# S5 branch of a hybrid decoder layer: halves swapped by DMA copies instead of products with a permutation, and the inner table laid out contiguously

## The chip, the cores and the metric

The kernel runs on one core of one Trainium2 chip. The metric is the device time of one execution in microseconds; several timed runs give a median. The core has five engines with queues of their own, each in order: TensorE (PE, with its weight loads as PEld), VectorE (DVE), ScalarE (ACT), GpSimd (POOL) and SyncE (SP). SP does no arithmetic here: it issues nearly all DMAs.

## What is computed

One decoder layer on 512 prompt tokens (plus 16 meta tokens in front) and 8 running sequences of 4 tokens, with model width 1024, in float32: a gated linear recurrence (HGRN2, 8 heads) and a grouped diagonal state-space branch (S5, 64 groups of 16 channels with 64 complex states each) are merged by gates, and an expert retrieval follows. The change is in the S5 branch, of which the reference says:

```
a_bar = exp(lam * delta)                      # per group and state, complex
b_bar = ((a_bar - 1.0) / lam) * (b_re + i b_im)
bu = einsum('gpc,nlgc->nlgp', b_bar, ug)      # 16 channels to 64 complex states
xs_t = a_bar * xs_(t-1) + bu_t                # a scan over the tokens
y = real(einsum('gcp,nlgp->nlgc', cc, xs)) + d_skip * ug
```

## The kernel before

The kernel works in stages, and within a stage a stream of weight tiles (class `Stream`, `run`) sets PE's order. A *job* multiplies one 128-column weight tile by all tokens: 24 steps of `gps` products (line 463) in two halves of 272 columns. After each quarter of a job (two of its eight k-steps, 12 products) `bg.tick` lets background tasks put their next step into the engines' queues. The order is thus fixed when the program is built: every engine takes its instructions in the order in which the code issues them, and waits where an operand isn't there yet or a buffer isn't free.

The weight tiles come through SP (`wraw`, two buffers). ACT makes a rounded copy `wh` of each, and POOL or DVE the remainder `wl`.

**Setup of the S5 constants** (`s5_setup`). It runs as a background task while PE does the projections and the HGRN2 heads. For each of 8 octets of groups it makes the matrices `AT` (inputs to chunk sums), `W` (states to outputs) and the block-Toeplitz table `T` (inputs to outputs within a chunk of 8 tokens). The small block `T7` is copied by 8 DMAs into a table tile of 128 x 1024 whose rows hold, per half octet, (s, c, g) with the group innermost; a DMA then stores the tile to DRAM (`Td`). Two table tiles take turns.

**The S5 units** (`s5_units`). 16 units of 4 groups each run as two background tasks, one for the even and one for the odd units; an even and an odd unit that go side by side are called a *pair* here. A unit has four steps, one tick each:

1. SP issues the loads `T`, `W`, `xs`, `xw0`, and then those of the task's next unit (`U`, `AT`, and the two rotation tables `rc` and `rs` in two halves each); PE makes `px` (line 740), ACT copies it to `X`, POOL sets up `d0`.
2. PE swaps the real and imaginary halves of the partitions of X by a product with the constant `perm` (line 755, tile `pxs`); DVE rotates (lines 760 to 762), scans over the chunks (line 767, result `z`) and starts the back rotation (line 768).
3. PE swaps the halves of z in the same way; DVE finishes the back rotation and writes the states `xs` (lines 778 to 780).
4. PE makes the outputs `py` from `U` with `T` and from `xs` with `W` (lines 785 and 786), ACT applies gelu, and ACT's queue stores `y` to DRAM (`Yd`).

`T`, `W` and `xs` have one buffer per task, `U`, `AT`, `rc` and `rs` have two. In step 4 the table is read as weights with a stride of four elements, because the group is innermost. The DMAs of SP and ACT signal their end over a set of semaphores that are used in turn; a DMA whose semaphore still belongs to an earlier DMA waits until that one has landed.

## Time and profile before

| | us |
|---|---|
| median of 3 runs | 2242.18 (2235.60 to 2245.61) |
| profiled execution, own time | 2232.85 |
| its span | 2230.7 |
| setup and heads, up to the S5 stretch | 0 to 499 |
| S5 stretch (gates and first branch products beside it) | 499 to 662 |
| the rest of the layer and the experts | 662 to 2230.7 |

Over the span PE is busy 95%, its weight loads 87%, DVE 71%, ACT 38% and POOL 36%; the chain of work that ended last runs over PE for 55% of the span and over DVE for 25%. A busy PE says little by itself, since matmuls overlap: what a product costs is read from start to start in the timeline. A row of the timeline gives the start, the time until the last of the merged instructions ended, the engine, the line, the tiles (out<-in) and the count; in brackets stand idle time before it and what ended it. A row of the windows gives the stretch, its length, the busy time of PE, PEld, DVE, ACT and POOL with instruction counts, PE's granted clock (1.00 is full speed), the DMA engines' busy share and GB/s.

### The profile page before, as it was taken

How to read it: one execution, taken by the hardware profiler on the slowest of the kernel's cores; microseconds unless marked ns; L12 is line 12 of the kernel's file. 1: busy time of each engine (PE TensorE's matmuls, PEld its weight loads, DVE VectorE, ACT ScalarE, POOL GpSimd, SP SyncE). 2: the span in 40 equal slices, each digit the busy share in tenths (PEclk: the TensorE clock that was granted, in tenths of full speed). 3: DMA queues.
4: the chain of work that ended last, by engine and by line, in shares of the span. 5: the costliest groups of instructions: out<-in, count | busy, mean ns of one | idle time of the engine just before them, and what ended most of it. 6: DMA issues, size and time to landing. Idle time of an engine off the chain costs nothing.

```text
span 2230.7 us, 34600 instructions
## 1 busy us (share of the span) xinstructions
PE 2108.4 (95%) x13085; PEld 1935.4 (87%) x13085; DVE 1587.8 (71%) x3108; ACT 848.2 (38%) x1583; POOL 811.6 (36%) x904
## 2 busy tenths in 40 slices
PE   7989999999999998999899999899999999999996
PEld 6978898898999998999799878788888888888885
DVE  6866677655335423799999678677877887787877
ACT  3323233232113323343477434333344343334343
POOL 3577762223443333564166111122222222222221
PEclk9989999999999998999999999999999999999998
DMA  5433444426644243232256989899989999888983
GB/s 151 117 96 102 127 133 139 136 99 183 193 144 129 86 154 111 91 100 72 97 227 264 333 305 344 305 333 326 332 314 325 334 335 334 307 328 309 336 302 138
DMA packets 199814, 478.90 MB, mean 215 GB/s; under 512 B 53440, under 2 KB 114752, under 8 KB 176096
## 3 DMA queue, kind: packets, MB, share of 16 engines
q1 hardware_dynamic: 169136, 278.50, 38.3%
q0 software_dynamic: 24752, 170.67, 20.7%
q10 hardware_dynamic: 5760, 27.53, 3.1%
q8 instruction: 103, 1.69, 0.3%
q14 instruction: 63, 0.52, 0.1%
HBM read 419.42 MB, written 54.46 MB: 212 GB/s over the span
## 4 chain that ended last, share of the span: by engine, by line
PE 55%; DVE 25%; issue 7%; ACT 7%; DMA 5%; POOL 1%; SPq 0%; DVEq 0%; POOLq 0%; ACTq 0%
PE gps L463 22%; PE eacc L1543 10%; DVE tlo L1472 5%; DVE uv L1348 5%; PE hps L1488 3%; PE hps L1490 3%; PE hps L1489 3%; DVE acc L1355 3%; PE pw L1423 3%; ACT thi L1464 3%; DMA traw<-in_uT 2%; PE aps L604 2%; DVE glo L477 2%; PE py L785 1%; ACT w L1350 1%
## 5 line engine op out<-in xcount | busy, mean ns | idle before, releaser
L463 PE MATMUL gps<-pr,wh 128*128 128x272 f32 (+1 forms) x3328 | 584.5, 298 | 4.4 <-DVE pr L477 3.8
L463 PEld LDWEIGHTS gps<-pr,wh 128*128 128x128 f32 x3328 | 481.9, 192 | 11.7 <-DVE pr L477 4.7
L1472 DVE TENSOR_TENSOR tlo<-traw,thi 128x1024 fp32r<-128x1024 f32 x241 | 299.1, 1241 | 139.9 <-ACT thi L1464 139.9
L1334 POOL DMA_INDIRECT uv<-in_uv,ei x128 | 176.9, 1382 | 598.4 <-DVE acc L1355 571.1
L1490 PE MATMUL hps<-pr,tlo 128*128 128x384 f32 x1024 | 348.8, 341 | 14.1 <-DVE tlo L1472 12.5
L1488 PE MATMUL hps<-pr,thi 128*128 128x384 f32 x1024 | 351.2, 343 | 8.4 <-ACT thi L1464 8.4
L463 PE MATMUL gps<-pr,wl 128*128 128x272 f32 (+1 forms) x1664 | 353.0, 292 | 1.1 <-POOL wl L429 0.7
L1489 PE MATMUL hps<-pr,thi 128*128 128x384 f32 x1024 | 345.0, 337 | 0.0
L429 POOL TENSOR_TENSOR wl<-wraw,wh 128x1024 fp32r<-128x1024 f32 x88 | 214.5, 2438 | 345.9 <-ACT wh L428 336.3
L1464 ACT CAST thi<-traw 128x1024 fp32r<-128x1024 f32 x256 | 266.0, 1040 | 37.9 <-PE eacc L1543 15.0
L463 PEld LDWEIGHTS gps<-pr,wl 128*128 128x128 f32 x1664 | 266.8, 192 | 1.7 <-POOL wl L429 1.2
L1543 PE MATMUL eacc<-thi,ghi 128*128 128x512 f32 x768 | 242.9, 397 | 6.1 <-ACT ghi L476 4.9
L1543 PE MATMUL eacc<-tlo,ghi 128*128 128x512 f32 x768 | 242.6, 397 | 4.2
L1543 PE MATMUL eacc<-thi,glo 128*128 128x512 f32 x768 | 238.1, 391 | 0.0
L1355 DVE SCALAR_TENSOR_TENSOR acc<-uv,w,acc 128x1024 f32<-128x1024 f32 x158 | 202.4, 1281 | 30.5 <-ACT w L1350 30.5
L1349 ACT ACTIVATE w<-w 128x1 f32<-128x1 f32 x160 | 32.5, 203 | 486.3 <-DVE uv L1348 486.3
L1490 PEld LDWEIGHTS hps<-pr,tlo 128*128 128x128 f32 x1024 | 193.3, 189 | 21.5 <-DVE tlo L1472 20.2
L1488 PEld LDWEIGHTS hps<-pr,thi 128*128 128x128 f32 x1024 | 193.8, 189 | 15.6 <-ACT thi L1464 10.5
L1489 PEld LDWEIGHTS hps<-pr,thi 128*128 128x128 f32 x1024 | 193.7, 189 | 3.6
L1348 DVE SCALAR_TENSOR_TENSOR uv<-uv,h 128x1024 f32<-128x1024 f32 x160 | 195.0, 1219 | 0.0
L1543 PEld LDWEIGHTS eacc<-tlo,ghi 128*128 128x128 f32 x768 | 141.2, 188 | 49.9 <-DVE tlo L1472 21.6
L1543 PEld LDWEIGHTS eacc<-thi,ghi 128*128 128x128 f32 x768 | 140.8, 188 | 42.5 <-ACT ghi L476 18.0
(403 smaller groups left out, 3026.7 us busy)
## 6 DMA issues: line engine op xcount, KB each, us to landing
traw<-in_uT SPq DMA_DIRECT2D x128, 512.0 KB
traw<-in_uv SPq DMA_DIRECT2D x128, 512.0 KB
wraw<-in_W SPq DMA_DIRECT2D x104, 512.0 KB
Wt<-wb ACTq DMA_DIRECT2D x24, 1024.0 KB
wt<-Wt SPq DMA_DIRECT2D x15, 1536.0 KB
st<-in_state_hgrn SPq DMA_DIRECT2D x8, 512.0 KB
out_o_hg_s<-st SPq DMA_DIRECT2D x8, 512.0 KB
Wd<-W SPq DMA_DIRECT2D x8, 512.0 KB
```

The costliest lines, as they stand in the source:

```text
L429: E.tensor_tensor(wl, r3, wh, ALU.subtract)
L463: mm(ps[:, b, :w], x[:, k], y[:, k, b * w : b * w + w], start=(k == 0 and x is wh and y is hi), stop=(k == KT - 1 and x is wl))
L1334: PO.indirect_dma_start(out=uvs[j], out_offset=None, in_=a["uv"], in_offset=bass.IndirectOffsetOnAxis(ap=ei[:, k : k + 1], axis=0))
L1348: V.scalar_tensor_tensor(out=uv[:, 0:D], in0=uv[:, 0:D], scalar=1.0, in1=h2, op0=ALU.mult, op1=ALU.mult, accum_out=w)
L1355: V.scalar_tensor_tensor(acc, uv[:, D:], w, acc, ALU.mult, ALU.add)
L1423: mm(pt[:, t], o2[:, t], o1[:, t], start=True, stop=True)
L1464: AC.copy(x, t)
L1472: (PO if kind == "u" and e < sum(AQ) else V).tensor_tensor(y, raws.pop((kind, e)), x, ALU.subtract)
L1488: mm(ps[:, :nt], x[:, ks], hi[:, k, cs], start=(k == 0), stop=False)
L1489: mm(ps[:, :nt], x[:, ks], lo[:, k, cs], start=False, stop=False)
L1490: mm(ps[:, :nt], y[:, ks], hi[:, k, cs], start=False, stop=(k == KT - 1))
L1543: mm(accs[d][:, b], l[:, ds_], r[:, b * 512 : b * 512 + 512], start=st, stop=en)
```

## The change

It has two parts.

- In a unit, the two products with `perm` are gone. The halves of X and of z are swapped by DMAs that SP issues, two for each (64 partitions to the other 64), into the new tiles `xw` and `zw`. The sign that `perm` carried is a per-partition constant `sgn`, applied by DVE in the multiplication with `rs`, now a scalar_tensor_tensor. The X swap is issued in step 1 behind the loads; the z swap in step 2 behind the scan.
- In the setup there is one table tile instead of two. ACT copies it into a tile `Tc` with the group outermost, and `Tc` is stored to DRAM. The load of `T` in a unit keeps its bytes, and `py` reads its weights contiguously.

```diff
-        T_["perm"] = const("perm", [P, P])
+        T_["sgn"] = const("sgn", [P, 1])
...
-        Ts = [q.tile([P, 2, 8, 16, 4], F32, name=f"T{i}") for i in range(2)]
-        for T in Ts:
-            PO.memset(T, 0.0)
+        T = q.tile([P, 2, 8, 16, 4], F32, name="T")
+        Tc = q.tile([P, 2, 4, P], F32, name="Tc")
+        PO.memset(T, 0.0)
...
         def store(o):
-            load(Td[o], Ts[o % 2].rearrange("p a s c g -> p a (s c g)"))
+            AC.copy(Tc, T.rearrange("p a s c g -> p a g (s c)"))
+            load(Td[o], Tc.rearrange("p a g n -> p a (g n)"))
...
-                load(Ts[o % 2][0 : 16 * (s + 1), :, s], T7[16 * (7 - s) : 128])
+                load(T[0 : 16 * (s + 1), :, s], T7[16 * (7 - s) : 128])
...
-            T = T.rearrange("p g n -> p (g n)").rearrange("p (n g) -> p g n", g=4)
...
             AC.copy(X, pxv)
+            xw, zw = st("xw", nch), st("zw", nch)
+
+            def swap(dst, src):
+                for x in range(2):
+                    load(dst[64 * x : 64 * x + 64], src[64 - 64 * x : 128 - 64 * x])
+
+            swap(xw, X[:, :, :nch])
...
-            yield
-
-            def swap(src):
-                t = pm.tile([P, 512], F32, name="pxs", tag="m")
-                tv = t[:, : 4 * nch].rearrange("p (g n) -> p g n", n=nch)
-                mm(tv, T_["perm"], src, start=True, stop=True)
-                return tv
-
-            xw = swap(X[:, :, :nch])
             V.tensor_tensor(Z, X[:, :, :nch], rc[:, :, 1 : nch + 1], ALU.mult)
-            V.tensor_tensor(t2, xw, rs[:, :, 1 : nch + 1], ALU.mult)
+            yield
+            V.scalar_tensor_tensor(t2, xw, T_["sgn"], rs[:, :, 1 : nch + 1], ALU.mult, ALU.mult)
...
             V.tensor_tensor_scan(z.rearrange(fl), d0.rearrange(fl), Z.rearrange(fl), 0.0, ALU.mult, ALU.add)
+            swap(zw, z)
...
-            zw = swap(z)
-            V.tensor_tensor(t2, zw, rs[:, :, 1 : nch + 1], ALU.mult)
+            V.scalar_tensor_tensor(t2, zw, T_["sgn"], rs[:, :, 1 : nch + 1], ALU.mult, ALU.mult)
```

On SP, at the third pair of units, stood before, from the odd task's load of its next `U` to the first load of the next pair:

```order
L104 DMA s_U_6158<-Ud0_103 128x328
L104 DMA s_AT_6159<-ATd_80 128x512
L104 DMA s_rc_6162<-Rd_82 64x268 x2
L104 DMA s_rs_6165<-Rd_82 64x268 x2
L104 DMA wraw_6233<-in_W 128x1024
L104 DMA s_T_6318<-Td_79 128x512
```

and stands now, from the even unit's X swap to the odd unit's z swap (`s_xw0` is a load as before, `s_xw` and `s_zw` are the swapped halves):

```order
L104 DMA s_xw_6161<-s_X_6159 64x4x66 x2
L104 DMA s_T_6174<-Td_79 128x512
L104 DMA s_W_6175<-Wd_81 128x512
L104 DMA s_xs_6176<-in_x0 128x4x8
L104 DMA s_xw0_6179<-in_x0w 128x32
L104 DMA s_U_6182<-Ud0_103 128x328
L104 DMA s_AT_6183<-ATd_80 128x512
L104 DMA s_rc_6186<-Rd_82 64x268 x2
L104 DMA s_rs_6189<-Rd_82 64x268 x2
L104 DMA s_xw_6199<-s_X_6197 64x4x66 x2
L104 DMA s_zw_6162<-s_z_6171 64x264 x2
L104 DMA s_zw_6200<-s_z_6209 64x264 x2
```

The X swap of each unit stands behind that unit's loads, and the z swaps of both units behind the X swap of the odd one.

On DVE, one pair of units reads before, from the even unit's rotation to its states:

```order
L761 TENSOR_TENSOR s_t2_6847<-pxs_6844,s_rs_6561 128x264
L762 TENSOR_TENSOR s_Z_6846<-s_Z_6846,s_t2_6847 128x264
L767 SCALAR_TENSOR_TENSOR s_z_6848<-s_d0_6799,s_Z_6846 128x264
L768 TENSOR_TENSOR s_zc_6849<-s_z_6848,s_rc_6558 128x264
L760 TENSOR_TENSOR s_Z_6876<-s_X_6838,s_rc_6599 128x264
L761 TENSOR_TENSOR s_t2_6877<-pxs_6874,s_rs_6602 128x264
L762 TENSOR_TENSOR s_Z_6876<-s_Z_6876,s_t2_6877 128x264
L767 SCALAR_TENSOR_TENSOR s_z_6878<-s_d0_6840,s_Z_6876 128x264
L768 TENSOR_TENSOR s_zc_6879<-s_z_6878,s_rc_6599 128x264
L900 SCALAR_TENSOR_TENSOR mix_5144<-mix_5144,gps_6737 128x544
L778 TENSOR_TENSOR s_t2_6847<-pxs_6912,s_rs_6561 128x264
L779 TENSOR_TENSOR s_xs_6776<-s_zc_6849,s_t2_6847 128x4x65
```

and now (the rows named SCALAR_TENSOR_TENSOR of line 766 are the scans):

```order
L760 SCALAR_TENSOR_TENSOR s_t2_6835<-s_xw_6826,c_sgn_336,s_rs_6584 128x264
L761 TENSOR_TENSOR s_Z_6834<-s_Z_6834,s_t2_6835 128x264
L766 SCALAR_TENSOR_TENSOR s_z_6836<-s_d0_6830,s_Z_6834 128x264
L768 TENSOR_TENSOR s_zc_6837<-s_z_6836,s_rc_6581 128x264
L760 SCALAR_TENSOR_TENSOR s_t2_6885<-s_xw_6876,c_sgn_336,s_rs_6634 128x264
L761 TENSOR_TENSOR s_Z_6884<-s_Z_6884,s_t2_6885 128x264
L766 SCALAR_TENSOR_TENSOR s_z_6886<-s_d0_6880,s_Z_6884 128x264
L768 TENSOR_TENSOR s_zc_6887<-s_z_6886,s_rc_6631 128x264
L899 SCALAR_TENSOR_TENSOR mix_5151<-mix_5151,gps_6764 128x544
L777 SCALAR_TENSOR_TENSOR s_t2_6835<-s_zw_6827,c_sgn_336,s_rs_6584 128x264
L778 TENSOR_TENSOR s_xs_6803<-s_zc_6837,s_t2_6835 128x4x65
```

The operations stand in the same order, but read tiles that DMAs write; the first rotation (`s_Z<-s_X`) of both units has moved ahead of this piece. As before, the even unit's states come behind the odd unit's scan.

## Rows read from the trace of the kernel before

**Rows 1.** Windows: busy us (instructions), clock, DMA share, GB/s; S5 stretch

```profile
499.00:662.00 163.00, 156.62 (x1067) 149.96 (x1065) 75.65 (x162) 35.47 (x59) 72.34 (x142) 0.98 0.59 175
```

**Rows 2.** Timeline of PE, one pair: start us, us, line, tiles, xcount

```profile
578.98 0.39 PE L786 MATMUL py<-s_xs,s_W 128*128 128x72 f32 x2
579.20 0.63 PE L785 MATMUL py<-s_U,s_T 128*128 128x72 f32 x2
579.67 0.39 PE L786 MATMUL py<-s_xs,s_W 128*128 128x72 f32 x2
...
583.62 0.75 PE L463 MATMUL gps<-pr,wh 128*128 128x272 f32 x4
584.21 0.42 PE L463 MATMUL gps<-pr,wl 128*128 128x272 f32 x2
...
585.21 1.01 PE L740 MATMUL px<-s_U,s_AT 128*128 128x82 f32 x8
...
587.60 0.61 PE L755 MATMUL pxs<-s_X,c_perm 128*128 128x264 f32 x2
587.85 0.85 PE L463 MATMUL gps<-pr,wh 128*128 128x272 f32 x4
588.54 0.41 PE L463 MATMUL gps<-pr,wl 128*128 128x272 f32 x2
```

**Rows 3.** Timeline of SP's queue: loads of one unit, start us, us

```profile
528.51 0.38 SPq L104 DMA_DIRECT2D s_T<-Td  x1
...
534.05 0.53 SPq L104 DMA_DIRECT2D s_T<-Td  x1
```

**Rows 4.** Tiles: ns min/median/max of SP's issues, first and last start

```profile
L104 SPq DMA_DIRECT2D s_rs<-Rd x32: 444/595/601, 494.8 to 633.5; - x32
...
L104 SPq DMA_DIRECT2D T<-T x64: 595/636/1508, 163.6 to 440.1; - x64
```

**Rows 5.** Chain that ended last: transfers in it; then landing of POOL's stores

```profile
502.87 3.95 DMA s_xs<-in_x
...
549.77 2.42 DMA s_rc<-Rd
...
DMA to landing us min/median/max: 1.7/1.9/2.1
```

**Rows 6.** Timeline of all engines, first pair: DVE and PE

```profile
504.94 0.43 DVE L761 TENSOR_TENSOR s_t<-pxs,s_rs 128x264 f32<-128x264 f32 x1
...
506.69 0.43 DVE L768 TENSOR_TENSOR s_zc<-s_z,s_rc 128x264 f32<-128x264 f32 x1
...
513.79 0.43 DVE L779 TENSOR_TENSOR s_xs<-s_zc,s_t 128x260 f32<-128x260 f32 x1
...
514.34 0.39 PE L786 MATMUL py<-s_xs,s_W 128*128 128x72 f32 x2
```

**Rows 7.** Timelines: SP's second `s_T` load, then PE's last pair

```profile
507.45 0.58 SPq L104 DMA_DIRECT2D s_T<-Td  x1
...
655.57 0.39 PE L786 MATMUL py<-s_xs,s_W 128*128 128x72 f32 x2
...
661.87 0.39 PE L786 MATMUL py<-s_xs,s_W 128*128 128x72 f32 x2
```

**Rows 8.** Waits in the stretch: us in total, times, longest; SP, then PE

```profile
SPq L104 <- DMA Yd<-s_y: 22.7, 9, 4.1
...
PE pxs L755 <- DVE s_z L767: 4.6, 7, 1.3
```

**Rows 9.** Timeline of PE, early in the stretch: idle time in brackets

```profile
513.12 0.74 PE L1030 MATMUL mps<-mr,k_e 32*128 32x272 f32 x2 [1.73 <-DVE og L1031]
...
516.98 1.25 PE L463 MATMUL gps<-pr,wh 128*128 128x272 f32 x4
```

**Rows 10.** Windows of the setup stretch; ACT's groups by form

```profile
260.00:320.00 60.00, 58.59 (x440) 55.92 (x441) 40.03 (x77) 19.81 (x41) 47.02 (x96) 0.94 0.38 126
...
L1425 ACT COPY wb<-pw 128x1024 f32<-128x1024 f32 x48 | 48.2, 1007 | 22.5 <-PE pw L1423 19.8 <-DMA Wt<-wb 2.5
```

More of the change, by code (lines that the diff above doesn't have):

```diff
@@ L1708, in layout @@
     r["ident"] = np.eye(P, dtype=np.float32)
-    pm_ = np.zeros((P, P), np.float32)
-    for p in range(64):
-        pm_[64 + p, p] = -1.0
-        pm_[p, 64 + p] = 1.0
-    r["perm"] = pm_
     sgn = np.ones((P, 1), np.float32)
```

## The prediction

> **What bounds the kernel now.** The table of busy time over the stretch in which the S5 units run (499 to 662 us) comes first: PE is busy 156.6 of 163.0 us, DVE and POOL under half, at a granted clock of 0.98 [rows 1]. So the stretch is as long as its PE work, and a matmul taken out of it is time won, unless something else comes late. PE's timeline then shows the pieces: groups of six `gps` products of the projection stream between the small S5 products `px`, `pxs` and `py` [rows 2]. Last comes SP's timeline. SP issues ten loads for each unit, 5.54 us from the first issue to the first of the next unit [rows 3], so 11.1 us for the two units of a pair. A pair takes (655.57 - 514.34) / 7 = 20.2 us, between the first `py` product on `s_xs` of the first and of the eighth pair [rows 6, 7]. SP has slack now only because nothing that it issues is needed in the same pair.
>
> **What the change takes off PE.** Each swap product and the slower start of the group behind it take 0.25 + (0.69 - 0.59) = 0.35 us [rows 2]; there are 32 of them (two for each of 16 units), 11.2 us. A pair of passes of `py` on `s_T` takes 0.47 us from start to start, one on the contiguous `s_W` 0.22 [rows 2]; 64 such pairs at 0.25 saved are 16.0 us. Waits of PE for `s_z` before the second swap were 4.6 us [rows 8]. Together up to 31.8 us, if nothing else becomes late. DVE's two multiplications become scalar_tensor_tensor on SBUF with the same 264 columns; I take them at the old 0.43 us [rows 6].
>
> **What it adds on SP.** Four DMAs a unit: two for X, two for z. The nearest rows are the half-tile loads of the rotation tables (64 partitions, nearly the same bytes; 0.60 us median) and the copies from SBUF to SBUF of the table (0.64 us) [rows 4]. I take 0.62 with the gap, so 4.96 us a pair; the low end is 0.45, the shortest rotation load. SP's issues alone come to 11.1 + 5.0 + about 0.4 for each weight tile, some 16.7 us a pair, still under 20.2. What decides is their place. SP takes its queue in order, and the X swap of a unit stands behind its ten loads. The first of these reloads `s_T`, which has one buffer, so it waits until `py` of the unit before has run. The z swaps of both units stand behind the X swap of the second, and on DVE the even unit's `s_xs` stands behind the odd unit's scan. So in each pair a chain forms that did not exist:
> - `py` of the even unit runs out, at the new pace: 7 passes in pairs of 0.22, 1.54 us [rows 2];
> - ten loads of the even unit, 5.54 [rows 3], and its X swap, 2 x 0.62 = 1.24;
> - ten loads of the odd unit, 5.54, and the first half of its X swap, 0.62;
> - the second half lands: between 1.9 us (POOL's small stores) and 3.95 us (a load in a burst); I take the rotation load's 2.42, the nearest in shape and queue [rows 5];
> - DVE: from t2 to the start of zc 1.75, zc 0.43, the even unit's t2 0.43, and from `s_xs` to the next `py` 0.55: 3.16 us [rows 6]; the even unit's z swap lands under this.
>
> Sum 20.1 us a pair. Three smaller terms come on top. SP waits for the landing of an earlier `Yd` store before reusing its semaphore (now 22.7 us in 9 waits, up to 4.1 [rows 8]): I take 0.6 a pair, 0 to 1.5. A weight tile sometimes stands between the two units' loads: 0.2, 0 to 0.7. And PE, which has some 16 us of work in such a pair, idles several us in one piece before each `py`. Some us after idle time of 1.73 us the present trace shows a `gps` group at 1.25 us [rows 9] instead of 0.75 [rows 2], the lower clock level; the products that lead to the next X then come late. I take 1.0, 0 to 2.5. That is 21.9 us a pair where 20.2 is spent now: **the chain through SP takes the place of PE's work**.
>
> Summed over the stretch: the first X swap can start only where the odd unit's `s_T` load starts now, 507.45 [rows 7]. Then 1.24 + 5.54 + 0.62 + 2.42 + 3.16 = 12.98 gives the first `py` on `s_xs` at 520.4 (now 514.3 [rows 6]). Six pairs at 21.9 lead to 651.8. The last pair has four loads a unit, four tenths of 5.54 us, and is led by PE's way to its X (about 6 us): 18 us, 669.8. From there `py`, a group of `gps` (1.59 [rows 2]) and the odd `py` take 4.9 us: 674.7, against 661.87 + 0.22 = 662.1 now [rows 7]. The stretch becomes **12.6 us longer**. PE is bound before and behind it, so this passes to the end.
>
> **The setup of the constants.** The table gets one buffer in place of two, and a copy of 128 x 1024 on ACT for each of 8 octets. A copy of that size on ACT takes 1.01 us [rows 10], 8.1 us in all. ACT is busy 19.8 of 60 us there [rows 10] and PE is nearly full, so I count a third, 3 us, for copies that the heads' work on ACT has to sit out; from 0 (all in ACT's idle time) to 9. The copy also waits for the table's DMAs of the octet before, issued some 20 us earlier; only for the last octet are they fresh. The strided read moves from PE to ACT: on PE the rows show 0.47 against 0.22 [rows 2]. The Trainium skill (SBUF — State Buffer, Door 1) says that consecutive accesses within a 16-byte line run at full rate and that a step to a new line costs; the trace agrees on PE, and by that rule ACT's copy would take an estimated 1.7 us instead of 1.0 and the setup term would be 5 us instead of 3.
>
> **Sum.** 12.6 + 3 = 15.6 us. On the profiled execution, 2232.85 us (span 2230.7 and 2.15 around it), that is 2248. The median of the runs is 2242.18, 9.3 us over the profiled one, so the forecast for a median is **2257 us**, +0.7%.
>
> **The rivals.**
> 1. *Faster: the swaps hide and PE stays the bound.* This needs issues much cheaper than 0.55 us, or swaps that don't wait behind the loads. Then the 31.8 us go, less 3 for the setup: 2213. For it: every engine but PE is under half busy [rows 1]. Against it: the 5.54 us of rows 3 and the swaps' place in the queue. [...]
> 2. *No change: the chain forms, but at its low end.* With 0.45 an issue and 1.9 to land, and none of the three small terms, the pair takes 20.1 - 0.34 - 0.17 - 0.52 = 19.1 us and the first `py` comes 1.0 earlier: the stretch is about 7 us shorter, 2235 without a setup cost. Up to 21.1 us a pair the result stays within 0.5%.
> 3. *Slower by much more: the chain with landings of 3.95 and the upper ends of the small terms.* 20.1 + 1.5 + 1.5 + 0.7 + 2.5 = 26.3 us a pair, some 44 us in all: about 2290. The forecast turns to the slow side from 21.1 us a pair on, where the chain costs more than 8 us over the stretch.
> 4. *The setup is the place:* ACT's copies delay heads at their full price, 9 us, with a chain at its low end. That ends within 0.5%, and is in 2.
> 5. *The weight load doesn't gain from the contiguous table.* The 16.0 us stay on PE; under the chain PE has slack, and this would add only the even `py`'s 0.75 us a pair.
>
> **How the numbers follow.** The forecast and the slower rival: 0.54. The chain near its low end, or with a cheap setup: 0.33. PE-bound, 2213: 0.13. About 0.5%, 11 us, is what a measurement of this kernel can tell from no change, and the chances by that bound are the same: faster 0.13, same 0.33, slower 0.54. The range leaves out rival 1 and the top of rival 3, and takes in the low end of the chain with a few us for the spread of the runs: 2228 to 2282.
>
> **What would show it.** In the changed kernel's trace: `py` passes on `s_T` at 0.22 us in a pair; PE idle for 3 us or more before the even unit's `py`, put down to DVE's `s_xs`; DVE waiting for the DMA of `s_xw`; SP without idle time from an even `s_T` load to the odd X swap; a pair of 21 to 23 us. I am wrong if pairs take 17 us or less, if SP's swap issues take far under 0.45 us, or if PE shows no wait for `s_xs`; and the setup term is wrong if the S5 stretch begins over 9 us later or not later at all.

## The result, and the profile after

| | before | after |
|---|---|---|
| median | 2238.89 us (2230.80 to 2245.61, 4 runs) | 2303.22 us (2299.92 to 2308.19, 4 runs) |
| profiled execution, own time | 2232.85 | 2300.84 |
| its span | 2230.7 | 2298.9 |
| first `px` to first `px` of the last unit | 145.0 | 200.3 |
| mean of a pair, first to eighth | 20.2 | 26.9 |

The ratio of the medians is 1.0295, interval 1.0267 to 1.0324: slower by 3%, where 0.7% was forecast. The direction was right, and so was the kind of mechanism, a chain through SP's queue in place of PE's work. The size was not, and the time lies 21 us over the upper end of the range.

The windows of the changed kernel over its S5 stretch, the counterpart of [rows 1] (columns as there):

```profile
516.00:733.00 217.00, 148.20 (x1000) 144.78 (x999) 84.72 (x162) 35.55 (x59) 71.58 (x142) 0.80 0.53 151
```

PE has 8 us less to do than before, although a part of it ran at a lower clock (0.80), and the stretch is 54 us longer: PE is no longer what bounds it. The waits in that stretch (us in total, times, longest), of PE and DVE:

```profile
DVE s_t L760 <- DMA s_xw<-s_X: 51.1, 12, 7.1
...
PE py L785 <- DVE s_xs L778: 43.4, 8, 9.7
```

And the waits of SP's queue there:

```profile
SPq L104 <- DVE s_zc L768: 23.4, 9, 3.5
SPq L104 <- POOL wl L430: 19.7, 5, 14.3
SPq L104 <- PE py L784: 13.8, 5, 3.7
SPq L104 <- ACT s_X L742: 13.7, 4, 5.7
SPq L104 <- POOL s_d L751: 9.3, 1, 9.3
SPq L104 <- DMA Yd<-s_y: 3.3, 5, 0.8
```

PE waits for `s_xs` ahead of every even `py`, and DVE waits for the X swap: the chain that the prediction drew. SP's wait for `Yd`, which it priced by [rows 8], nearly went. SP's wait for POOL's `wl` stayed, and now the swaps stand behind it. The 9.3 us put down to POOL's `s_d` are such a wait too: the weight tile's load that ends it starts at 657.78, when POOL's `wl` has run from 655.41 for 2.35 us.

One pair of the changed kernel in three timelines (start us, us, engine, line, tiles, count). PE's, from the even `py` to the even `px`:

```profile
599.51 0.70 PE L785 MATMUL py<-s_xs,s_W 128*128 128x72 f32 x2 [7.10 <-DVE s_xs L778]
600.00 0.63 PE L784 MATMUL py<-s_U,s_T 128*128 128x72 f32 x2
600.43 0.64 PE L785 MATMUL py<-s_xs,s_W 128*128 128x72 f32 x2
...
602.52 1.25 PE L464 MATMUL gps<-pr,wh 128*128 128x272 f32 x4
...
604.02 0.88 PE L464 MATMUL gps<-pr,wh 128*128 128x272 f32 x4
...
604.99 0.34 PE L784 MATMUL py<-s_U,s_T 128*128 128x72 f32 x2
605.16 0.39 PE L785 MATMUL py<-s_xs,s_W 128*128 128x72 f32 x2
605.38 0.39 PE L784 MATMUL py<-s_U,s_T 128*128 128x72 f32 x2
...
606.72 1.06 PE L740 MATMUL px<-s_U,s_AT 128*128 128x82 f32 x8
607.58 0.75 PE L464 MATMUL gps<-pr,wh 128*128 128x272 f32 x4
...
608.41 0.66 PE L464 MATMUL gps<-pr,wh 128*128 128x272 f32 x4
```

SP's, from the even unit's loads to the odd X swap:

```profile
602.38 0.33 SPq L104 DMA_DIRECT2D s_T<-Td  x1
...
609.23 1.31 SPq L104 DMA_DIRECT2D s_xw<-s_X  x2
611.74 0.34 SPq L104 DMA_DIRECT2D wraw<-in_W  x1
612.18 0.38 SPq L104 DMA_DIRECT2D s_T<-Td  x1
...
617.55 1.30 SPq L104 DMA_DIRECT2D s_xw<-s_X  x2
```

And POOL, DVE and PE from the odd unit's `t2` to the next even `py`:

```profile
619.21 2.35 POOL L430 TENSOR_TENSOR wl<-wraw,wh 128x1024 fp32r<-128x1024 f32 x1
620.64 1.22 DVE L760 SCALAR_TENSOR_TENSOR s_t<-s_xw,c_sgn,s_rs 128x264 f32<-128x264 f32 x1 [6.22 <-DMA s_xw<-s_X]
...
624.61 0.70 PE L785 MATMUL py<-s_xs,s_W 128*128 128x72 f32 x2 [8.20 <-DVE s_xs L778]
```

The passes on `s_T` and on `s_W` take the same 0.22 us in the odd `py` (604.99, 605.16, 605.38), as forecast for the contiguous table. The even `py` and the `gps` group behind it come after 7.10 us without work, and run at 0.43 us a pass and 1.50 a group (602.52 to 604.02), in place of 0.22 and 0.83 (607.58 to 608.41): half the speed. The granted clock was 0.50 from 599.5 to 604, the 1.2 GHz level. A weight tile keeps the odd unit's loads from 610.54 to 612.18, and `t2` takes 1.22 us beside POOL's `wl`.

Over the seven intervals between the eight even `py`, the pair falls into four legs. Each is the mean of seven differences of start times: the first `py` on `s_xs` of the even unit, SP's even X swap, SP's odd X swap, DVE's `t2` of the odd unit, and the next even `py`. The rows e9 to e17 are experiments told below. All legs come from one profiled execution of each kernel; that of e14 and of e16 was the quickest of theirs (2285.41 us for a median of 2295.72, 2251.38 for 2258.97), so their gains in this table are upper figures.

| us | `py` to even swap | to odd swap | to odd `t2` | to next `py` | pair |
|---|---|---|---|---|---|
| prediction's chain | 7.1 | 6.8 | 3.0 | 3.2 | 20.1, with small terms 21.9 |
| after | 12.6 | 7.0 | 3.2 | 4.1 | 26.9 |
| e9, weight tiles off SP | 11.4 | 6.6 | 4.0 | 3.9 | 25.9 |
| e10, loads behind the swaps | 11.2 | 4.3 | 3.8 | 5.3 | 24.6 |
| e14, `wl` off POOL | 12.1 | 6.7 | 3.1 | 3.7 | 25.6 |
| e16, e10 and e14 together | 10.7 | 4.1 | 3.2 | 3.8 | 21.8 |
| e17, e16 and PE kept busy | 9.1 | 4.1 | 3.4 | 5.2 | 21.7 |

Three legs came out as drawn, to within 1 us. The first is 5.5 us longer, more than all that a pair is off.

In the pair shown above SP's loads end at 609.14, after X (608.32), as the prediction had it. In four of the seven intervals it is the other way round: SP is through with its loads and stands for X, the 13.7 us of the table of waits. One of them (SP's last loads of the even unit, ACT's copy of X, SP's even X swap):

```profile
579.76 1.24 SPq L104 DMA_DIRECT2D s_rs<-Rd  x2
585.36 0.43 ACT L742 COPY s_X<-px 128x328 f32<-128x328 f32 x1 [2.01 <-PE px L740]
585.82 1.30 SPq L104 DMA_DIRECT2D s_xw<-s_X  x2
```

### The profile page after: what moved, and what is told of

It is laid out like the page before. It is cut to its first block, busy times and chain, and to the rows that moved or that the text cites. A ratio compares the mean times of both kernels' runs of the same rounds, so it can differ in the third digit from the quotient of the medians.

```text
span 2298.9 us, 34624 instructions
## 1 busy us (share of the span) xinstructions
PE 2113.1 (92%) x13021; PEld 1944.0 (85%) x13021; DVE 1600.0 (70%) x3108; ACT 863.6 (38%) x1591; POOL 809.7 (35%) x903
## 4 chain that ended last, share of the span: by engine, by line
PE 50%; DVE 26%; issue 8%; ACT 7%; DMA 5%; SPq 2%; POOL 1%; DVEq 0%; ACTq 0%; POOLq 0%
PE gps L464 22%; PE eacc L1542 7%; DVE uv L1347 5%; DVE tlo L1471 5%; PE hps L1487 3%; PE hps L1489 3%; DVE acc L1354 3%; PE hps L1488 3%; ACT thi L1463 3%; PE pw L1422 3%; SPq L104 2%; DVE glo L478 2%; PE aps L605 2%; DMA traw<-in_uT 1%; ACT w L1349 1%
## 5 line engine op out<-in xcount | busy, mean ns | idle before, releaser
L464 PEld LDWEIGHTS gps<-pr,wh 128*128 128x128 f32 x3328 | 489.3, 195 | 10.4 <-DVE pr L478 4.1
L1489 PEld LDWEIGHTS hps<-pr,tlo 128*128 128x128 f32 x1024 | 193.9, 189 | 20.3 <-DVE tlo L1471 19.1
L1542 PEld LDWEIGHTS eacc<-tlo,ghi 128*128 128x128 f32 x768 | 141.2, 188 | 49.6 <-DVE tlo L1471 21.8
```

Of the source, the lines that this page charges most:

```text
L464: mm(ps[:, b, :w], x[:, k], y[:, k, b * w : b * w + w], start=(k == 0 and x is wh and y is hi), stop=(k == KT - 1 and x is wl))
L1489: mm(ps[:, :nt], y[:, ks], hi[:, k, cs], start=False, stop=(k == KT - 1))
L1542: mm(accs[d][:, b], l[:, ds_], r[:, b * 512 : b * 512 + 512], start=st, stop=en)
```

## The experiments

Ratios are to the kernel before, run on the same chip beside each. "Px to px" is from the first `px` of the first unit to the first of the last.

### Each part alone

`e1_swap_only` takes the swaps without the table, `e2_layout_only` the table without the swaps.

```diff
...
-            AC.copy(Tc, T.rearrange("p a s c g -> p a g (s c)"))
-            load(Td[o], Tc.rearrange("p a g n -> p a (g n)"))
+            load(Td[o], Ts[o % 2].rearrange("p a s c g -> p a (s c g)"))
...
+            T = T.rearrange("p g n -> p (g n)").rearrange("p (n g) -> p g n", g=4)
```

That is e1, from the changed kernel; e2 is the kernel before with these lines the other way round.

> The swaps by DMA alone; the table keeps two tiles, is stored with the group innermost and is read with the stride. Theory Q (the S5 stretch grew by 54 us because the swaps stand behind the loads in SP's queue, and the setup grew by 16.7 us because of ACT's copy of the table): the setup term goes, so the S5 stretch begins near 499 again; the stretch itself stays at about 217 us, plus up to 1 us a pair because the even unit's py is back at 0.47 us for two passes. Time about 2290 to 2300. Theory C (the copy of the table in the setup and the swaps share one cause, a lower TensorE clock on this profile, and the swaps cost only the forecast 13 us): about 2255 to 2265.

> The contiguous table alone; the halves are swapped by products with perm, as before. Theory Q: the setup stretch is longer by 15 to 17 us (eight ACT copies of 2.05 us, nearly all felt), the S5 stretch is shorter by 13 to 16 us (64 pairs of passes at 0.22 in place of 0.47). Time 2235 to 2245, no change. Rival S (the setup's 16.7 us came from the swaps or from a disturbed clock and not from the copy): the setup is longer by 3 us or less, time about 2225.

Measured: e1 2305.61 us, ratio 1.0323 (1.0302 to 1.0345), pair 27.6 us; e2 2234.38 us, ratio 0.9993 (0.9977 to 1.001), pair 18.2. The whole loss is the swaps'. The contiguous table takes 14 us out of the S5 stretch where PE is the bound (px to px 131.2 against 145.0), and in the setup it gives 10 of them back by the profiled executions (the medians of e2 and of the kernel before are equal); under the swaps' chain it comes out as 0.7 us a pair.

Where the S5 stretch starts is the first of the two times in these rows on the products `px` (count, ns min/median/max, first and last start, shape). The changed kernel:

```profile
L740 PE MATMUL px<-s_U,s_AT x128: 233/275/283, 516.0 to 717.0; 128*128 128x82 f32 x128
```

e1, the swaps alone:

```profile
L740 PE MATMUL px<-s_U,s_AT x128: 232/275/421, 509.3 to 714.6; 128*128 128x82 f32 x128
```

e2, the table alone:

```profile
L740 PE MATMUL px<-s_U,s_AT x128: 232/275/283, 509.6 to 641.6; 128*128 128x82 f32 x128
```

e3 (below), the changed kernel up to this point:

```profile
L740 PE MATMUL px<-s_U,s_AT x128: 233/275/439, 508.9 to 665.3; 128*128 128x82 f32 x128
```

Against 499.3 before, e1 starts 10 us later without any copy of the table, and e3 starts 7 us earlier than the changed kernel, with the same instructions so far. So the changed kernel's 16.7 us have two causes. One is the clock in single executions. Two windows of the changed kernel (columns as in [rows 1]):

```profile
340.00:360.00 20.00, 19.99 (x132) 18.70 (x133) 10.15 (x21) 7.27 (x14) 3.68 (x2) 0.83 0.40 139
360.00:380.00 20.00, 16.50 (x96) 15.89 (x95) 14.28 (x22) 6.06 (x7) 3.07 (x2) 0.72 0.44 153
```

The same two of e3:

```profile
340.00:360.00 20.00, 19.15 (x148) 17.56 (x149) 12.92 (x24) 9.55 (x18) 4.28 (x2) 1.00 0.52 177
360.00:380.00 20.00, 15.68 (x129) 15.15 (x128) 16.50 (x28) 6.37 (x9) 4.82 (x2) 1.00 0.36 122
```

This dip is in 10 of the 19 profiles, in kernels with and without the copy, and costs 7 to 10 us where it is (516.0 against 508.9; e1 against before). The other cause is the copy, seen in e2's timeline of ACT and PE:

```profile
444.54 1.99 ACT L346 COPY Tc<-T 128x1024 f32<-128x1024 f32 x1 [4.57 <-DMA T<-T]
...
447.90 0.27 ACT L657 COPY h_Sc<-psm 128x128 f32<-128x128 f32 x1
448.22 0.80 PE L665 MATMUL po<-h_qF,h_Sc 128*128 128x128 f32 x2 [4.68 <-ACT h_Sc L657]
```

The last octet's copy waits 4.57 us for its fresh DMAs, the heads' copy of `h_Sc` stands behind it on ACT, and PE waits 4.68 us for that and then runs at a granted clock of 0.57 (448 to 452 us). e8 puts that one copy six ticks later, and e5 does without a copy.

```diff
+        for _ in range(6):
+            yield
         store(7)
```

That is e8, from e2. And e5, from the kernel before:

```diff
-        Ts = [q.tile([P, 2, 8, 16, 4], F32, name=f"T{i}") for i in range(2)]
+        Ts = [q.tile([P, 2, 4, 8, 16], F32, name=f"T{i}") for i in range(2)]
...
-                load(Ts[o % 2][0 : 16 * (s + 1), :, s], T7[16 * (7 - s) : 128])
+                load(Ts[o % 2][0 : 16 * (s + 1), :, :, s], T7[16 * (7 - s) : 128])
```

> The kernel before with the contiguous table alone, made without ACT's copy: two table tiles as before, with the group outermost, and the DMAs that fill them write it so, in runs of 16 elements in place of 64. Theory Z (of the setup's delay with the copy some 8 us are the last octet's copy, behind which ACT's work for the heads stands, and the rest was a lower clock in that one profile): no delay from 430 to 470 us, the S5 stretch 13 to 14 us shorter than before, time about 2220 to 2224, ratio 0.994. Rival R (the short runs make the table's DMAs slow enough to hold up SP's queue in the setup, the weight tiles among it): 2230 or more.

> The contiguous table alone with ACT's copy, as in e2_layout_only, but the last octet's copy is put into the queues six ticks later, when the DMAs that it waits for have landed. Theory Z (the last octet's copy costs about 8 us, since ACT waits for fresh DMAs there with the heads' work behind it; the other seven cost next to nothing): no wait of ACT for the table's DMAs, 7 to 9 us less than e2_layout_only, time about 2226. Rival A (all eight copies cost their 2 us each on the path of the heads): within 2 us of e2_layout_only.

Measured: e5 2227.32 us, ratio 0.9949 (0.9927 to 0.9971); e8 2227.53 us, ratio 0.994 (0.9916 to 0.9965). Both beat the kernel before by half a per cent, and so the changed one by more. In e5's profile S5 begins at 512.7 us, but that execution has the dip (0.83 and 0.75 in the two windows), so it does not show what e5's setup costs. In e8 no wait of ACT for the table's DMAs is left, and S5 begins at 502.4:

```profile
L742 PE MATMUL px<-s_U,s_AT x128: 232/275/283, 502.4 to 634.1; 128*128 128x82 f32 x128
```

The one copy cost 7 us (against e2), the seven others 3 us at most together (against before). Rival A fell.

### The dependence alone, and another queue

`e3_no_wait` issues every swap and lets `t2` read X and z, so the swap is left out of the arithmetic; `e4_swaps_act` issues the swaps from ACT; `e6_loads_act` issues the next unit's six loads from ACT.

```diff
-            V.scalar_tensor_tensor(t2, xw, T_["sgn"], rs[:, :, 1 : nch + 1], ALU.mult, ALU.mult)
+            V.scalar_tensor_tensor(t2, X[:, :, :nch], T_["sgn"], rs[:, :, 1 : nch + 1], ALU.mult, ALU.mult)
...
-            V.scalar_tensor_tensor(t2, zw, T_["sgn"], rs[:, :, 1 : nch + 1], ALU.mult, ALU.mult)
+            V.scalar_tensor_tensor(t2, z, T_["sgn"], rs[:, :, 1 : nch + 1], ALU.mult, ALU.mult)
```

That is e3; e4, in `swap`, and e6, where the loads are called (all from the changed kernel):

```diff
-                    load(dst[64 * x : 64 * x + 64], src[64 - 64 * x : 128 - 64 * x])
+                    AC.dma_start(dst[64 * x : 64 * x + 64], src[64 - 64 * x : 128 - 64 * x])
```

```diff
-                nxt = loads(units[n_ + 1])
+                nxt = loads(units[n_ + 1], AC.dma_start)
```

> The changed kernel with all its swap DMAs issued where they are, but t2 reads X and z themselves instead of xw and zw, so the output differs; DVE no longer waits for a swap to land. SP's issues are all still there. Theory Q (place in the queue matters only because DVE waits for it): PE is the bound again, clock 0.97 or more in the S5 stretch, the stretch about 163 - 31 = 132 to 140 us, time about 2225 to 2235 with the setup's 16 us. Rival I (SP's issue time alone, 22 DMAs a pair of units and its waits for X, z, wl and Yd, cannot keep up): the pair stays at 23 us or more and the time over 2270.

> The changed kernel with the four swap DMAs of a unit issued by ACT's queue instead of SP's. They no longer stand behind the loads. Theory Q: the chain loses twenty loads of a pair (11 us); a pair takes 17 us or less, DVE's wait for the X swap falls to about 2.5 us each, the time is 2235 to 2255 (the setup's 16 us stay). Rival L (the landing of two swaps in a row for each unit, about 3 us each, and the in-order wait of DVE on it are enough to starve PE, wherever they are issued): the pair stays above 21 us and the time above 2270; ACT's queue, held up by the scan's result, then delays gelu and the weight copies too.

> The changed kernel with the six loads of a task's next unit issued by ACT's queue; T, W, xs, xw0, the weight tiles and all swaps stay on SP. Theory O (SP's issue time is the bound: in the run in which DVE doesn't wait, SP is without a gap for 20.9 us a pair and the T loads come late): SP has some 12 us of issues a pair, the pair falls to 17 us or less, the clock in the S5 stretch is 0.93 or more, the stretch 125 to 140 us from the first to the last px, time 2225 to 2245. Rival L (the landings of the swaps and the in-order waits of DVE are enough by themselves): the pair stays over 20 us, the time over 2260.

Measured: e3 2257.83 us, ratio 1.0115 (1.0086 to 1.0144), pair 21.7; e4 2271.25 us, 1.0154 (1.0128 to 1.0181), pair 23.4; e6 2311.55 us, 1.0326 (1.0277 to 1.0374), pair 28.6. Theories Q and O failed in all three: e4 and e6 came out within rival L's bounds, e3 between theory Q and rival I. From the first `px` to the first of the last unit e3 takes 155.7 us, 45 less than the changed kernel: so much is the wait of DVE for the swaps. It is still 24 us over e2's 131.2, and its waits of PE show why there is a second floor under the first:

```profile
PE py L785 <- DVE s_xs L778: 10.4, 5, 3.0
PE py L784 <- DMA s_T<-Td: 9.8, 5, 4.3
```

With nobody waiting for a swap, SP's issues still fill the pair (twenty loads, eight swap DMAs and a weight tile or two, nearly all at 0.33 to 0.65 us, some 17 us with the gaps, and 23.3 us of waits for `Yd` over the stretch; the 22 of the expectation counts two half tiles as one), and `T` comes late. So in this order on this queue the swaps would have cost time even if nobody had waited for them.

On ACT the DMAs stand ahead of other things. e4 won 32 us against the changed kernel, but PE still waited 29.0 us for `s_xs`, in 8 waits. In e6, ACT issues a unit's loads ahead of the copy of its `px`; the first of these copies in the timeline below comes 3.6 us after its product has ended (PE, then ACT's queue and ACT):

```profile
599.20 1.06 PE L740 MATMUL px<-s_U,s_AT 128*128 128x82 f32 x8
...
602.55 1.20 ACTq L716 DMA_DIRECT2D s_rs<-Rd  x2
603.85 0.44 ACT L742 COPY s_X<-px 128x328 f32<-128x328 f32 x1 [4.03 <-DMA s_rc<-Rd]
```

### What stands in the chain

`e9_wraw_pool` loads the stretch's weight tiles through POOL, right behind the subtraction that frees their buffer. `e10_loads_late` moves the next unit's loads behind the z swap. e11 is both; e12 is both with those loads on ACT.

```diff
-                load(raw, a["W"][self.jobs[i][0]])
+                self.q(raw, a["W"][self.jobs[i][0]])
...
-            s.rate = O_RATE
+            s.rate, s.q = O_RATE, PO.dma_start
```

That is e9, where `q` is `load` again behind the stretch; and e10:

```diff
-            if n_ + 1 < len(units):
-                nxt = loads(units[n_ + 1])
             px = pm.tile([P, 512], F32, name="px", tag="m")
...
             swap(zw, z)
+            if n_ + 1 < len(units):
+                nxt = loads(units[n_ + 1])
```

> The changed kernel with the weight tiles of the stretch loaded through POOL's queue, where each stands right behind the subtraction that frees its buffer, so that SP no longer waits for wl. Theory W (in the changed kernel SP's waits for POOL's wl, 19.7 us in all and 14.3 in one piece ahead of the second pair, hold up the unit loads and with them the swaps): the interval between the first and the second even py falls from 34.3 to some 24 us, the stretch from the first to the last px from 201 to 180 to 185 us, time 2280 to 2287. Rival M (the loads would then wait for something else that is as late, py or the scan): 2295 or more.

> The changed kernel with the six loads of a task's next unit issued by SP behind the unit's z swap instead of ahead of its X swap. SP issues the same DMAs in another order. Theory P (the place in the queue: twelve issues, some 6 us a pair, go out of the chain from py to the next py): a pair of 20 to 22 us in place of 25 to 28, limited by SP's issues, which are some 16.6 us a pair plus its waits; time 2260 to 2275. Rival I (SP's total of issues and waits decides, not their order): within 10 us of the changed kernel, 2293 to 2310.

> Both: the weight tiles through POOL's queue and the next unit's loads behind the z swap on SP. If theories W and P both hold and add up: 2240 to 2258, a pair of 18 to 20 us. If SP's total of issues is the bound in the end, the two together give no more than the better of them.

> The weight tiles through POOL's queue, and the next unit's loads through ACT's queue behind the place of the z swap (so that they do not stand ahead of ACT's copies of px). SP keeps T, W, xs, xw0 and the swaps, some 10 us of issues a pair. Theory O (SP's issues are the last bound): a pair of 17 us or less, PE the bound again, the stretch from the first to the last px 125 to 140 us, time 2222 to 2240. Rival L (the landings of the swaps and the in-order DVE are enough by themselves to starve PE): a pair of 19 us or more, time over 2250.

Measured: e9 2297.76 us, ratio 1.0267 (1.0229 to 1.0305), px to px 193.8; e10 2278.82 us, 1.02 (1.0164 to 1.0236), px to px 179.4; e11 2268.84 us, 1.0162 (1.0131 to 1.0193), pair 23.5; e12 2300.77 us, 1.0311 (1.0266 to 1.0356), pair 26.1. e9 took SP's wait on `wl` away and won 1 us a pair, less than theory W had: SP then waited for `py` and X instead (24.7 and 20.3 us in the stretch), as its rival M had it. By the time alone e9 can't be told from the changed kernel, whose interval of the ratio overlaps e9's. e10 won 2.3 us a pair, less than theory P had, most of it in the second leg; the first, where six of the loads had stood too, is still 11.2. A pair of e10 in SP, PE and ACT, from SP's last load of the even unit to its X swap:

```profile
567.24 0.51 SPq L104 DMA_DIRECT2D s_xw<-in_x0w  x1
...
572.60 1.91 PE L738 MATMUL px<-s_U,s_AT 128*128 128x82 f32 x16
573.69 0.43 ACT L740 COPY s_X<-px 128x328 f32<-128x328 f32 x1 [0.99 <-PE px L738]
574.15 1.32 SPq L104 DMA_DIRECT2D s_xw<-s_X  x2
```

SP has done its four loads at 567.75 and does nothing for 6.4 us, until X is there: from the even `py` at 563.04, PE needs some 10 us for it, two or three `gps` groups, the odd `py` and `px`. The last leg grew, and e16 takes that back (below). e11 (both) took its second branch: its time, whose interval overlaps e10's, is no better than e10's by more than the noise. e12 came out as its rival L had it and did not free the chain: ACT's loads stood ahead of ACT's weight copies, and both queues stood between two issues for a DMA still in flight, so that the two issues of an odd X swap, 0.60 us each, took up to 3.90 us together.

### The clock, and POOL beside DVE

e7 and e13 put twenty and twelve products whose results are never read ahead of the even `py` (e13 from the third pair on), so that PE has work in a part of its wait; e15 does e13's in e11. `e14_wl_act` makes `wl` on ACT, as a copy of the whole weight tile: the subtraction is left out, so the stream's products come out doubled, and not only changed in their low-order parts as the expectation says. e16 is e10 with e14's edit, e17 is e16 with e13's products.

```diff
+            if units[0] == 0 and n_ >= 2:
+                for _ in range(12):
+                    mm(py[:, : 4 * nch].rearrange("p (g n) -> p g n", n=nch), r["AT"][:, 0], X[:, :, :nch], start=True, stop=True)
             for g in range(4):
                 mm(pyv[:, g], T[:, g], U[:, g, m0 : m0 + ny], start=True, stop=False)
```

That is e13, ahead of the products of `py`; and e14, where `act` is true for the stretch only:

```diff
-            E.tensor_tensor(wl, r3, wh, ALU.subtract)
+            if self.act:
+                AC.copy(wl, r3)
+            else:
+                E.tensor_tensor(wl, r3, wh, ALU.subtract)
```

> The changed kernel with twenty more products (the form of the former swap products, results never read) on PE ahead of each even unit's py, where PE waits 7 to 9 us: 5 us of added work at full clock, in time that PE spends waiting. Theory K (the wait costs more than itself, since what follows it runs at the lower clock: py 2.9 in place of 1.54 us and the products up to the next px): the granted clock of the S5 stretch rises from 0.80 to 0.90 or more, a pair is 2 to 4 us shorter, the time 2275 to 2290. Rival N (the lower clock after the wait lies beside SP's issues and costs nothing, or the added products don't lift it): the time stays at 2300 to 2310, or grows by up to 40 us where the products outlast the wait.

> The changed kernel with twelve more products (results never read, 5.5 us at full clock) ahead of the even unit's py, from the third pair on, where PE waits 7 to 10 us. In e7_warm twenty took 9.1 us, as long as the wait, and stood in the first pairs too, behind DVE's og. Theory K (the lower clock after the wait is a large part of the missing 5 us a pair): the even X swap starts 7 to 8.5 us after the even py instead of 9.7 to 11.3, the pairs from the third on fall from 26.4 to 22 to 24 us, time 2283 to 2293. Rival D (the clock is recovered under SP's loads and costs nothing): the pairs stay at 25 us or more, time 2298 or more.

> The changed kernel where, within the stretch, wl is a plain copy made by ACT (1.05 us a weight tile) and not the subtraction on POOL (2.4 us), so the output differs in the low-order parts. Theory D (DVE's operations beside POOL's subtraction take 1.2 to 2.7 us in place of 0.49 and stand in the chain, and SP's wait on wl costs 1 us a pair): t2 and the scan at 0.49 and 0.72 throughout, pairs 1.5 to 3 us shorter, time 2280 to 2292. Rival K (only the clock matters): within 7 us of e9_wraw_pool's 2298, and t2's mean unchanged in its effect on the pair.

> e11_wraw_pool_late (weight tiles through POOL, next unit's loads behind the z swap) with the twelve added products of e13_warm12. If the clock is the last large term, the pairs from the third on fall from 23.1 to 19 to 21 us and the time is 2245 to 2258, although PE does 33 us more of matmuls than in e11_wraw_pool_late. If the clock costs nothing, 2266 or more.

> The changed kernel with the next unit's loads behind the z swap on SP, and wl a plain copy made by ACT within the stretch (so the output differs in the low-order parts). If the two terms add up, the pairs take 21 to 23 us (e10_loads_late: 24.6, e14_wl_act: 25.6 on the mean) and the time is 2260 to 2270; if one hides the other, no less than e10_loads_late's 2279 less 3.

> e16_late_wlact with the twelve added products of e13_warm12 from the third pair on. If the clock is a term of the chain that POOL's subtraction hid in e15_wraw_late_warm, pairs from the third on fall by 2 to 3 us against e16_late_wlact (to 19 to 20.5) and the time by 10 to 15; if the products only take PE's time, the time is that of e16_late_wlact or up to 10 us more.

Measured: e7 2317.65 us, ratio 1.0359 (1.0312 to 1.0405); e13 2304.66, 1.0316 (1.0285 to 1.0347); e14 2295.72, 1.0277 (1.0246 to 1.0307); e15 2278.76, 1.019 (1.0158 to 1.0222); e16 2258.97, 1.0111 (1.0079 to 1.0142); e17 2251.16, 1.0075 (1.0047 to 1.0102).

e7's products took 9.1 us instead of 5, and those of the first two pairs came behind `og`, so it says little. In e13 the clock held in two of the five pairs, where the first leg was 9.2 and 8.1 us (9.7 and 10.2 in the same pairs of the changed kernel), and the time did not move: by itself the clock was worth nothing measurable, and theory K fell in that form. A pair of e15 shows where such a gain went, on DVE and POOL:

```profile
647.62 3.37 DVE L764 TENSOR_TENSOR_SCAN s_z<-s_d,s_Z 128x264 f32<-128x264 f32 x1
648.07 2.35 POOL L430 TENSOR_TENSOR wl<-wraw,wh 128x1024 fp32r<-128x1024 f32 x1
```

The scan, 0.72 us otherwise, took 3.37 beside the subtraction. Three of e15's sixteen scans took 3.4 us, where one of e11's took 2.96 and the rest at most 0.98. With the subtraction off POOL (e14), `t2` fell. The group of its instructions in the changed kernel (busy us, mean ns, idle before):

```profile
L760 DVE SCALAR_TENSOR_TENSOR s_t<-s_xw,c_sgn,s_rs 128x264 f32<-128x264 f32 x16 | 15.7, 980 | 51.1 <-DMA s_xw<-s_X 51.1
```

And in e14:

```profile
L763 DVE SCALAR_TENSOR_TENSOR s_t<-s_xw,c_sgn,s_rs 128x264 f32<-128x264 f32 x16 | 7.9, 493 | 53.7 <-DMA s_xw<-s_X 53.7
```

That is worth up to 1.3 us a pair alone (e14's time misses theory D's range, and its interval overlaps the changed kernel's) and up to 2.8 once the loads are out of the way (e16 against e10, where the times are apart too): the terms hid each other. It is not SP's wait for the weight tile that went: in e14 SP waits for ACT's `wl` instead, 15.1 us in 5 waits. In e17 the first leg is 7.7 us from the third pair on, against 10.0 in e16; PE then has no wait for `s_xs` over 0.5 us, so its added 33 us of products set the pair. The time is 8 us lower than e16's, although the intervals overlap. The part of the leg that is PE's own, from the even `py` to the end of ACT's copy of X, is 7.4 us there, as in e2 (7.3 in the same pairs), against 9.8 in e16. So the clock is a real term of the first leg, 2.3 us there. What it is worth in the changed kernel's time stays open, since keeping PE busy takes time of its own.

## Why the prediction missed, step by step

- **PE's relief** was right where it was measured: 0.22 us for either pass, and 14 us for the table alone where 16.0 were forecast. What the swap products cost (11.2 forecast) no run shows by itself. Rival 5 fell, and its 0.75 us a pair under the chain came out as 0.7 (e1 against the changed kernel).
- **The chain through SP takes the place of PE's work:** right, with PE waiting 43.4 us for `s_xs` in 8 waits, and 51.1 us of DVE for the X swap. The first even `py` on `s_xs` comes 22.2 us after the first `px`, where 21.1 was forecast.
- **The issues, the landing and DVE's part** held: X swaps at 0.65 a DMA with the gap (0.62 forecast), 3.2 us to `t2` (3.0), 4.1 to `py` (3.2).
- **The failed step is the first leg:** the even unit's `py` at 1.54 us, its ten loads at 5.54, then its X swap. It took X as ready when the loads were through, and gave PE's way to X no term. The leg is 12.6 us, 5.5 more, of which the trace shows three parts. SP's loads start 1.3 us later, since `py` runs at half speed. In the first and the fifth interval they start another 10.3 and 5.2 us later, behind the weight tile, 2.2 a pair on the mean. And in four of seven intervals SP then stands for X, 2.0 a pair. Ten loads took 6.1 us, near the forecast, and the four of the last interval 1.8.
- **Two ways of one length:** from the even `py` to the end of the loads it is 10.6 us on the mean, to the end of ACT's copy of X 10.8, and the swap waits for the later of the two. That is why e10, without six of the loads, still has 11.2 in this leg, and e9, without the weight tile, 11.4. In e2, with the same table and a granted clock of 0.99 (525 to 641 us), PE's way is 7.8 us. In the kernel before it was slack, since X was needed only later; the prediction used it ("about 6 us") for the last pair alone. Its own sign, SP without idle time from an even `s_T` load to the odd X swap, did not show.
- **The clock, "1.0, 0 to 2.5" a pair:** the even `py` takes 3.0 us and not 1.54, and e17 puts 2.3 us of the first leg to the clock. The term was small by half, though within its range, and it stands inside the failed step.
- **The weight tile, "0.2, 0 to 0.7" a pair:** the failed price with a row to be had. In the waits of SP's queue in the kernel before, over its S5 stretch, the one on `wl` was 19.4 us, up to 14.4 in one piece:

```profile
SPq L104 <- POOL wl L429: 19.4, 3, 14.4
```

PE was busy 156.6 of 163.0 us there, so it can have cost little, and [rows 8] showed only the wait for `Yd`. In the changed kernel SP stands from 536.57 to 550.93 for it, since ACT's weight copy stands behind gelu of a late `py`; the interval of that pair is 34.3 us. On the way to the swap the wait is 2.2 us a pair, as told; since X is late too, taking it away won 1 us (e9).

- **DVE's multiplications "at the old 0.43 us":** `t2` for X takes 0.98 on the mean. Before, one operand came from PSUM (`pxs`), and the same line took 0.43, also in the two of sixteen that ran beside a `wl`. The Trainium skill (SBUF — State Buffer, Who interferes with whom) says that a DVE instruction with two SBUF inputs contends with a GpSimd instruction that reads SBUF, and that one with at most one such input, outside its two-port modes, does not. The trace agrees: `t2` takes 1.22 us beside `wl`, and 0.49 with `wl` off POOL. The kernel before shows both sides of it within one `wl`:

```profile
587.77 2.38 POOL L429 TENSOR_TENSOR wl<-wraw,wh 128x1024 fp32r<-128x1024 f32 x1 [5.95 <-PE gps L463]
588.25 0.43 DVE L761 TENSOR_TENSOR s_t<-pxs,s_rs 128x264 f32<-128x264 f32 x1 [1.77 <-PE pxs L755]
588.72 1.72 DVE L762 TENSOR_TENSOR s_Z<-s_Z,s_t 128x264 f32<-128x264 f32 x1
```

The multiplication with an operand in PSUM runs at its 0.43; the next instruction, with both inputs in SBUF, takes 1.72 and ends after `wl`. Moving the operand of `t2` to SBUF put it into the second case. By e14 all of DVE's delays beside POOL's subtraction together cost up to 1.3 us a pair; `t2` has the largest part of them.
- **The setup, 3 us, 0 to 9:** about 10 us, by the starts of e2 (10.3 after before's) and e3 (9.6), neither with the dip; e8 shows 7.2 of them to be the last octet's copy. That is just over the upper end, and by the prediction's own sign (S5 over 9 us later) the term was wrong: it priced the copies, and the last octet's fresh DMAs, which it named and gave no price, were most of the cost. The copies take 2.05 us, not 1.01. The prediction had estimated 1.7 by the rule that it took from the Trainium skill (SBUF — State Buffer, Door 1), a rule without a number; the trace agrees that the strided read costs, and is above that estimate. The 16.7 us seen in the profile are this and the dip of the clock, which is not the change's.
- **Sum.** Of the 52 us by which the profiled execution is over the forecast for it, 39 are the seven pairs, 14 the setup with the dip; the rest cancels.
- Rival 3, 26.3 us a pair and some 2290, was near the size, but by other terms: not landings of 3.95 and `Yd`, but the first leg. Rivals 1 and 2 fell: in e3, where no swap is waited for, a pair still takes 21.7 us.

Of the 6.7 us a pair over the kernel before, the runs name the loads' place (2.3), POOL beside DVE (up to 1.3 alone, up to 2.8 behind that) and SP's wait on `wl` (1.0, e9). These overlap, and e16 with two of them gone is still 1.1% slower than before. What the rest consists of stays open.

## What to carry to other kernels

When a step is moved from the engine that bounds to a queue, walk the whole new loop, the way back through the old engine too: what was slack while that engine was full (here PE's way to X) becomes a leg of the chain. Price every wait that a queue already has ahead of the moved step, above all those that cost nothing today. And an extra copy on an engine costs where it waits on fresh data with other work behind it; moving the one copy that does, or writing the layout with the DMAs that are there anyway, kept the gain of the contiguous table, half a per cent.

## What the runs showed of the hardware

- A DVE scan of 128 x 264 took 3.37 us and a `t2` up to 2.96 us (e15) beside POOL's subtraction of 128 x 1024, where they take 0.72 and 0.49 alone. With one operand in PSUM the same multiplication took 0.43 us beside it.
- SP's DMA issues took 0.33 to 0.65 us each (but for 7 of 201 in e3, the longest 1.48), so that the 29 or 30 of a pair (twenty loads at 11.1 us [rows 3], eight swap DMAs at 0.46 to 0.64, the weight tiles and the gaps) took some 17 of its 21.7 us in e3.
- ACT's copy of 128 x 1024 that reads with a step of four elements took 2.05 us; a contiguous one of that size takes 1.01 [rows 10].
- With the same instructions, two executions were granted a clock of 1.00 and of 0.72 to 0.83 over the same 40 us of the heads, a difference of 7 us.
